# Where the modulation sums stand in the first attention of a two-layer decoder

## The chip, the cores and the metric

One core of a Trainium2 chip runs the whole forward pass of a two-layer decoder trunk as one program. The metric is the device time of one execution in microseconds. A core has five engines that run their own instruction queues in order and wait for each other by semaphores: TensorE (PE, matrix products), VectorE (DVE), ScalarE (ACT), GpSimd (POOL) and SyncE (SP, which here only issues DMAs).

## The reference, cut to what matters

The trunk works on 256 tokens of width 1024 in fp32. Every layer is a SwiGLU FFN, an attention, and another FFN; each sub-layer's input is normalised and modulated by a shift and a scale, and its output by a gate, which come from one vector `c`. Layer 0 uses differential attention with 8 heads, the stage of this study:

```python
c_act = jax.nn.silu(c)
mod = c_act @ ada_w[layer] + ada_b[layer]
sh1, sc1, g1, sh2, sc2, g2, sh3, sc3, g3 = jnp.split(mod, N_MOD, axis=-1)
...
h = modulate(rms_norm(x, norm_g[layer, 1]), sh2, sc2)
qkv = h @ w_qkv
...
logits = jnp.einsum('bqhmd,bkhmd->bhmqk', qb, k).astype(jnp.float32) * scale + bias
logits = jnp.where(rel >= 0, logits, -jnp.inf)
p = jax.nn.softmax(logits, axis=-1)
w = p[:, :, 0] - lam * p[:, :, 1]
return jnp.einsum('bhqk,bkhe->bqhe', w.astype(v.dtype), v)
...
o = rms_norm(o, subln_g) * (1 - lambda_init)
return o.reshape(b, s, A_V_WIDTH) @ w_o
```

The products `c_act @ ada_w` (18 sections of 1024 outputs over both layers, and two for the shared keys and values) don't depend on the tokens. They can be worked out at any time until the sub-layer that uses them.

## The kernel before, in words

**Products in three parts.** Activations are held transposed (feature on the partition, 256 tokens on the free axis). Each fp32 operand is split in a high and a low part of a faster type: `HH`/`HL` for activations, `wh`/`wl` for weights, and a product is three matmuls (`wh`·`HH`, `wl`·`HH`, `wh`·`HL`; `mm3`). A weight piece of 128 x 1024 comes from HBM into one of 6 `raw` tiles (SP issues the DMA), ACT makes `wh` (`cp_part`, a CAST), and DVE makes `wl` = raw - wh (`sub_part`, in one of 5 tiles). As soon as the subtraction is done, SP may load the next piece into that `raw` tile. A piece of 24 matmuls keeps PE busy for about 2.7 us.

**Modulation sums.** One modulation sum (`ada_block`) is one DVE instruction over a 128 x 1024 half of an `ada` tile, which multiplies by silu(c) and sums along the row: 128 outputs of a section. 160 of them are needed. Three `ada` tiles of 1 MB are kept; after the second half of a tile its next load is issued (`ada_dma`), in the same SP queue as the weights. `need(...)` makes whatever is still missing where a section is used; the first attention has to leave behind the sections (0,5), (0,6) and (0,7).

**What sets the order.** The engines' queues are written in program order by a planner inside the kernel. It keeps an estimated time per engine (`InOrder`). After each matmul, `work` calls `bg`, which gives ACT and DVE weight splitting and, in the mode "run", modulation sums for which a credit has built up; the credit grows with PE's work at the rate `PACE` of the stage (0.74 in the first attention). Before an instruction that would wait by the estimate, `fill_dve` and `fill_act` put the same kinds of work into the gap; `plain(f, ...)` writes an instruction sequence without such fillings, and `dve.plainly` one instruction.

**The first attention** (`attention_a`). `late_pairs` makes queries and keys of heads 0 and 1. Then, while PE works through the value projection (`v_proj`) and the other heads' query and key projections (`pair_proj`, 48 matmuls each, tile `pqk`), the heads go through a pipeline, one group per head. `group(t)` puts on PE the scores of head t (`s`), the transposes of head t-1's weights (`pw`), the value products of head t-2 and the transposes of head t-3's result (`po`). Behind that follow `exps(t)`: four reads of the scores by DVE (`nl`<-`s`,`g`, which add the bias and take the row's extreme `nm`), each followed by an exponential on ACT; `squares` on ACT and `inv_rms` (DVE row `ss`, then a power on POOL); and `out_split` (ACT `oh`, DVE `ol`). `combine(t)` forms the difference of the two softmaxes on DVE (a reciprocal and five scalings `rs`, `nl`), which PE transposes in the next group. `scale_o` scales the result on ACT (`on`). From head 7 on PE fills the time with the output projection (`OutProj`, tile also `pw`), and `finish` ends the stage with the update of x, whose halves feed the next FFN.

In before, only the reads of head 7 and its combination stand under `plain`: in the other heads `fill_dve` may put a `wl` or a sum between two reads.

Of the kernel before, what the change touches and what calls it, by code (L numbers as in the profile page):

```python
# [22 lines left out]
AH = 8  # L23
# [17 lines left out]
CP_FIT = 0.9  # L41
DVE_FIT = 0.6
NFILL = 1
PACE = [0.62, 0.74, 0.62, 0.38, 0.76, 0, 0.74]
NRAW = 6
NLO = 5
NHI = 6
# [57 lines left out]
def trunk(ctx, tc, a, out):  # L105
# [4 lines left out]
    dve = InOrder(tc, nc.vector, 0.08, 1 / 960)  # L110
# [17 lines left out]
    def bbank(name):  # L128
        return pp.tile([P, 512], F32, tag="tb", name=name)
# [3 lines left out]
    def plain(f, *args):  # L133

        r = []
        act.plainly(lambda: dve.plainly(lambda: r.append(f(*args))))
        return r[0]
# [40 lines left out]
    ada_at = {}  # L178
# [4 lines left out]
    ada_done = [0]  # L183
# [742 lines left out]
    def pair_proj(src, dst, name):  # L926

        pq = mmbank(name)
        blk = take(src)
        for k in range(NC):  # L930
            for b in range(2):
                mm3(pq[:, b * 256:b * 256 + 256], blk(k * 256 + b * P), hn[k],
                    k == 0 and b == 0, k == NC - 1)
            if k == NC - 1:
                act.copy(dst, pq)
            yield k, NC
# [37 lines left out]
    for k in range(0, NC, 2):  # L974
# [7 lines left out]
        if k % 4:  # L982
            i = k // 4
# [75 lines left out]

    pace[0] = PACE[0]  # L1060
    ffn(0, 0, None, ((0, 1), (0, 0)), ((0, 4), (0, 3)))
# [3 lines left out]
    def attention_a():  # L1065
# [7 lines left out]
        def qk_tile(hd):  # L1073
            return kp.tile([P, 512], F32, tag="w512a", name=f"qk{hd}")
# [4 lines left out]
        def load_g(hd):  # L1079
            g = cp_.tile([P, S], F32, tag=("hidh10", "hidl10")[hd % 2], name=f"g{hd}")  # L1080
            nc.gpsimd.dma_start(g, bass.AP(skew.tensor, skew.offset + hd * P * UW + 127, [[UW - 1, P], [1, S]]))
            gs[hd] = g
# [7 lines left out]
        def scores(hd):  # L1090
            sb = [sbank(f"s{hd}_{m}") for m in range(2)]
            for qt, (c0, w) in enumerate(QT):
                for m in range(2):
                    rows = slice(m * HD, m * HD + HD)
                    mm(sb[m][:, c0:c0 + w], qk[hd][rows, qt * P:qt * P + P], qk[hd][rows, 256:256 + w],
                       start=True, stop=True)
            return sb

        def exps(hd, sb):
            g = gs[hd]  # L1100
            nl = []
            nm = kp.tile([P, 4], F32, tag="nm", name=f"nm{hd}")
            sm = kp.tile([P, 4], F32, tag="sm", name=f"sm{hd}")
            for m in range(2):
                s = sb[m]
                n_ = cp_.tile([P, 384], F32, tag=f"hidh{4 + 2 * (hd % 2) + m}", name=f"nl{hd}_{m}")
                nl.append(n_)
                for qt, (c0, w) in enumerate(QT):
                    cc = 2 * m + qt
                    dve.tensor_tensor_reduce(  # L1110
                        n_[:, c0:c0 + w], s[:, c0:c0 + w], g[:, S - w:], -0.125, BIG,
                        ALU.add, ALU.min, accum_out=nm[:, cc:cc + 1])
                    act.activation(n_[:, c0:c0 + w], n_[:, c0:c0 + w], AF.Exp,
                                   bias=nm[:, cc:cc + 1], scale=-1.0,
                                   accum_out=sm[:, cc:cc + 1])
            st[hd], sms[hd] = nl, sm

        def combine(hd):
            nl, sm = st[hd], sms[hd]
            rs = kp.tile([P, 4], F32, tag="rs", name=f"rs{hd}")  # L1120
            dve.reciprocal(rs, sm)
            dve.tensor_scalar(rs[:, 2:4], rs[:, 2:4], nlam, None, op0=ALU.mult)
            for qt, (c0, w) in enumerate(QT):
                cs = slice(c0, c0 + w)
                dve.tensor_scalar(nl[1][:, cs], nl[1][:, cs], rs[:, 2 + qt:3 + qt], None, op0=ALU.mult)
                dve.scalar_tensor_tensor(nl[0][:, cs], nl[0][:, cs], rs[:, qt:qt + 1], nl[1][:, cs],
                                         op0=ALU.mult, op1=ALU.add)
            st[hd] = nl[0]
            if hd + 2 < AH:
                load_g(hd + 2)  # L1130

        def weights_t(hd):
            pw = abank(f"pw{hd}")
            for b in range(3):
                pe.transpose(pw[:, b * P:b * P + P], st[hd][:, b * P:b * P + P], ident)
            return pw

        def values(hd, po):
            wt = st[hd]
            vs = slice((hd % 4) * P, (hd % 4) * P + P)  # L1140
            v0, v1 = va[0][hd // 4][:, vs], va[1][hd // 4][:, vs]
            mm(po[:, 0:P], wt[:, 0:P], v0, start=True, stop=True)
            mm(po[:, P:2 * P], wt[:, P:2 * P], v0, start=True, stop=False)
            mm(po[:, P:2 * P], wt[:, 2 * P:3 * P], v1, start=False, stop=True)

        def squares(hd, po):
            on = kp.tile([P, 256], F32, tag="w512b", name=f"on{hd}")
            ss = kp.tile([P, 2], F32, tag="ss", name=f"ss{hd}")
            for qt in range(2):
                act.activation(on[:, qt * P:qt * P + P], po[:, qt * P:qt * P + P], AF.Square,  # L1150
                               accum_out=ss[:, qt:qt + 1])
            st[hd] = (po, on, ss)

        def inv_rms(hd):
            ss = st[hd][2]
            dve.tensor_scalar(ss, ss, 1.0 / P, EPS, op0=ALU.mult, op1=ALU.add)
            nc.gpsimd.tensor_tensor(ss, ss, half, op=ALU.pow)
            InOrder.ready[(ss.tensor.name, 0)] = dve.t + 1.0

        def scale_o(hd):  # L1160
            po, on, ss = st[hd]
            for qt in range(2):
                act.activation(on[:, qt * P:qt * P + P], po[:, qt * P:qt * P + P], AF.Copy,
                               scale=ss[:, qt:qt + 1])
            st[hd] = on

        def out_t(hd, pz):
            for qt in range(2):
                pe.transpose(pz[:, qt * P:qt * P + P], st[hd][:, qt * P:qt * P + P], ident)

        def out_split(hd, pz):
            oh, ol = o[hd]
            act.activation(oh, pz, AF.Identity, scale=subg)
            dve.scalar_tensor_tensor(ol, pz, subg, oh.bitcast(F32), op0=ALU.mult, op1=ALU.subtract)

        def group(t):

            hs, hw, hv, ho = (h if 0 <= h < AH else None for h in (t, t - 1, t - 2, t - 3))
            bank = bbank(f"po{t}") if hv is not None or ho is not None else None
            sb = scores(hs) if hs is not None else None  # L1180
            pw = weights_t(hw) if hw is not None else None
            if hv is not None:
                values(hv, bank[:, :256])
            if ho is not None:
                out_t(ho, bank[:, 256:])
            if hw is not None:
                wt = cp_.tile([P, 384], F32, tag=f"hidh{8 + hw % 2}", name=f"wt{hw}")
                act.copy(wt, pw[:, :384])
                st[hw] = wt
            if hs is not None:  # L1190
                plain(exps, hs, sb) if hs == AH - 1 else exps(hs, sb)
            if hv is not None:
                squares(hv, bank[:, :256])
                inv_rms(hv)
            if ho is not None:
                plain(out_split, ho, bank[:, 256:]) if ho == AH - 1 else out_split(ho, bank[:, 256:])

        def after(t):
            if t < AH:
                plain(combine, t) if t == AH - 1 else combine(t)  # L1200
            if 0 <= t - 2 < AH:
                scale_o(t - 2)

# [16 lines left out]
        for t in range(2, AH):  # L1220
            qk.append(qk_tile(t))
            for i, _ in enumerate(pair_proj("wqk", qk[t], f"pqk{t}")):
                if t > 2 and i == 2:
                    group(t - 1)
                if t > 2 and i == 5:
                    combine(t - 1)
                if t > 2 and i == 7:
                    scale_o(t - 3)
        step(4)
# [8 lines left out]

    pace[0] = PACE[1]
    op, rest = attention_a()  # L1240
    op.finish((0, 5), ((0, 7), (0, 6)), rest, (3, 2, 2, 1, 0, 0, 0, 0))
    pace[0] = PACE[2]
    ffn(0, 1, "late", ((0, 7), (0, 6)), (("kv", 1), ("kv", 0)), at=3)
# [10 lines left out]
    for t in fgs:  # L1254
        nc.gpsimd.memset(t.bitcast(F32), 0.0)
    pace[0] = PACE[3]
    rstd = late_pairs("wkk", kT, (("kv", 1), ("kv", 0)), AF.Exp)
# [54 lines left out]

    pace[0] = PACE[4]
    ffn(1, 0, "ready", None, ((1, 4), (1, 3)))
# [142 lines left out]

    pace[0] = PACE[5]
    op, rest = attention_b()
# [135 lines left out]
```

## Time and profile before

| | us |
|---|---|
| three runs, median (lowest to highest) | 965.37 (964.58 to 965.74) |
| the profiled execution | 964.25 |
| its span, first to last instruction | 962.5 |
| first attention in the span (chain: from the first lp to the last output projection) | 193.4 to 300.7 |
| 18 modulation sums in 193 to 300 us on DVE | 22.7, 1.28 each |
| 31 wl subtractions in 193 to 300 us on DVE | 37.0, 1.22 each |

A row of the view in order of time gives its start and length in us, engine, line, operation, output<-inputs, shapes, and in brackets the engine's idle time before it with what ended it. Rows of one engine overlap by some hundredths of a microsecond, so spacing is read from start to start. Nearly every instruction has the line 100, that of the helper which records it; the tiles' names tell them apart. Names in the profile have no buffer numbers: `nl` stands for all heads, and heads are told by the order. Matmuls are pipelined, their rows (0.28 us) overlap, and PE's time is read from the spacing: 0.11 us for 128 x 256.

### The profile page before, as it was taken

How to read it: one execution, taken by the hardware profiler on the slowest of the kernel's cores; microseconds unless marked ns; L12 is line 12 of the kernel's file. 1: busy time of each engine (PE TensorE's matmuls, PEld its weight loads, DVE VectorE, ACT ScalarE, POOL GpSimd, SP SyncE). 2: the span in 40 equal slices, each digit the busy share in tenths (PEclk: the TensorE clock that was granted, in tenths of full speed). 3: DMA queues.
4: the chain of work that ended last, by engine and by line, in shares of the span. 5: the costliest groups of instructions: out<-in, count | busy, mean ns of one | idle time of the engine just before them, and what ended most of it. 6: DMA issues, size and time to landing. Idle time of an engine off the chain costs nothing.

```text
span 962.5 us, 20495 instructions
## 1 busy us (share of the span) xinstructions
PE 953.4 (99%) x8088; PEld 930.1 (97%) x8088; DVE 821.8 (85%) x1369; ACT 556.4 (58%) x908; POOL 75.6 (8%) x119
## 2 busy tenths in 40 slices
PE   8999999999999999999999999999999999999997
PEld 7999999988999999999997999999998899999997
DVE  8989988889999999878899988889988799555575
ACT  6575654575877645455577554445567766554432
POOL 0000001100112000000000000000064014300000
PEclk9999999999999999999999999999999999999999
DMA  9998989968767699878959899989895437987641
GB/s 367 414 368 310 375 313 324 364 220 309 270 212 251 214 381 381 293 282 314 337 187 370 310 343 333 342 290 317 320 315 168 118 127 220 269 169 248 192 148 44
DMA packets 69661, 267.89 MB, mean 278 GB/s; under 512 B 9572, under 2 KB 10413, under 8 KB 59454
## 3 DMA queue, kind: packets, MB, share of 16 engines
q1 hardware_dynamic: 66060, 259.35, 76.9%
q0 software_dynamic: 3072, 6.92, 2.5%
q8 instruction: 63, 1.03, 0.4%
q10 hardware_dynamic: 434, 0.33, 0.1%
q14 instruction: 32, 0.26, 0.1%
HBM read 264.42 MB, written 2.66 MB: 277 GB/s over the span
## 4 chain that ended last, share of the span: by engine, by line
PE 98%; DVE 1%; DMA 0%; ACT 0%; issue 0%; SPq 0%; DVEq 0%; ACTq 0%
PE po L100 26%; PE pg L100 22%; PE pu L100 22%; PE pw L100 5%; PE pv L100 5%; PE pf L100 5%; PE lp L100 4%; PE pqk L100 3%; PE lq L100 1%; PE lu L100 1%; PE lg L100 1%; PE pk L100 1%; PE wb L100 1%; PE sb L100 1%; PE s L100 1%; PE wa L100 0%
## 5 line engine op out<-in xcount | busy, mean ns | idle before, releaser
L100 ACT CAST wh<-raw 128x1024 fp32r<-128x1024 f32 (+1 forms) x360 | 347.7, 975 | 206.7 <-PE pu L100 87.0
L100 DVE TENSOR_TENSOR wl<-raw,wh 128x1024 fp32r<-128x1024 f32 (+1 forms) x360 | 401.8, 1132 | 74.2 <-ACT sg L100 25.0
L100 DVE CUSTOM_DVE_ANT_0 ada<-ada,cact,vecs 128x1024 f32<-128x1024 f32 x144 | 182.7, 1279 | 0.0
L100 PE MATMUL pg<-HH,wl 128*128 128x256 f32 x608 | 167.9, 276 | 0.0
L100 PE MATMUL pu<-HH,wh 128*128 128x256 f32 x608 | 167.9, 276 | 0.0
L100 PE MATMUL pg<-HH,wh 128*128 128x256 f32 x608 | 167.9, 276 | 0.0
L100 PE MATMUL pu<-HL,wh 128*128 128x256 f32 x608 | 167.9, 276 | 0.0
L100 PE MATMUL pg<-HL,wh 128*128 128x256 f32 x608 | 167.9, 276 | 0.0
L100 PE MATMUL pu<-HH,wl 128*128 128x256 f32 x608 | 167.9, 276 | 0.0
L100 PE MATMUL po<-hidh,wh 128*128 128x256 f32 x528 | 145.7, 276 | 0.0
L100 PE MATMUL po<-hidh,wl 128*128 128x256 f32 x528 | 145.7, 276 | 0.0
L100 PE MATMUL po<-hidl,wh 128*128 128x256 f32 x528 | 145.7, 276 | 0.0
L100 PEld LDWEIGHTS pg<-HH,wh 128*128 128x128 f32 x608 | 114.1, 188 | 0.0
L100 PEld LDWEIGHTS pg<-HH,wl 128*128 128x128 f32 x608 | 114.1, 188 | 0.0
L100 PEld LDWEIGHTS pg<-HL,wh 128*128 128x128 f32 x608 | 114.1, 188 | 0.0
L100 PEld LDWEIGHTS pu<-HH,wh 128*128 128x128 f32 x608 | 114.1, 188 | 0.0
L100 PEld LDWEIGHTS pu<-HL,wh 128*128 128x128 f32 x608 | 114.1, 188 | 0.0
L100 PEld LDWEIGHTS pu<-HH,wl 128*128 128x128 f32 x608 | 114.1, 188 | 0.0
L100 PEld LDWEIGHTS po<-hidh,wl 128*128 128x128 f32 x528 | 99.1, 188 | 0.0
L100 PEld LDWEIGHTS po<-hidl,wh 128*128 128x128 f32 x528 | 99.1, 188 | 0.0
L100 PEld LDWEIGHTS po<-hidh,wh 128*128 128x128 f32 x528 | 99.1, 188 | 0.0
L100 ACT CAST hidh<-hf 128x512 fp32r<-128x512 f32 x44 | 27.3, 621 | 47.3 <-DVE hf L100 47.3
(244 smaller groups left out, 1878.3 us busy)
## 6 DMA issues: line engine op xcount, KB each, us to landing
raw<-in_win SPq DMA_DIRECT2D x176, 512.0 KB, 5.6
ada<-in_ada SPq DMA_DIRECT2D x79, 1024.0 KB, 7.3
raw<-in_wout SPq DMA_DIRECT2D x48, 384.0 KB, 5.4
raw<-in_wout SPq DMA_DIRECT2D x48, 320.0 KB, 5.1
raw<-in_wqk SPq DMA_DIRECT2D x16, 512.0 KB, 4.9
raw<-in_wo SPq DMA_DIRECT2D x16, 512.0 KB, 4.7
raw<-in_wlast SPq DMA_DIRECT2D x16, 512.0 KB, 4.3
raw<-in_wv SPq DMA_DIRECT2D x8, 512.0 KB, 8.1
```

Source lines behind the costliest of these rows:

```text
L100: return self.tc.keep_in_program_order(f(*args, **kw))
```

## The change

Every head's reads are now written under `plain`, so neither a wl nor a sum nor a CAST comes between them. The credit's rate in the first attention goes to 0, and a function `sums` writes up to two modulation sums, without a planner's condition other than that sections which this stage must leave behind are still missing. It is called behind the combinations of heads 0, 1 and 7 (`after`) and, in the loop over heads 2 to 7's projections, at step 5, which is behind `combine(t - 1)`; for t = 2 no combination stands there. That makes nine calls and 18 sums.

```diff
-PACE = [0.62, 0.74, 0.62, 0.38, 0.76, 0, 0.74]
+PACE = [0.62, 0, 0.62, 0.38, 0.76, 0, 0.74]
...
             if hs is not None:
-                plain(exps, hs, sb) if hs == AH - 1 else exps(hs, sb)
+                plain(exps, hs, sb)
...
+        due = 2 * max(ada_at[m] for m in ((0, 5), (0, 7), (0, 6)))
+
+        def sums():
+            for _ in range(2):
+                if ada_done[0] < due:
+                    dve.plainly(ada_block)
+
         def after(t):
             if t < AH:
                 plain(combine, t) if t == AH - 1 else combine(t)
+            if t in (0, 1, AH - 1):
+                sums()
             if 0 <= t - 2 < AH:
                 scale_o(t - 2)
...
                 if t > 2 and i == 5:
                     combine(t - 1)
+                if i == 5:
+                    sums()
                 if t > 2 and i == 7:
                     scale_o(t - 3)
```

PE's order is the same in both. DVE's differs from head 0's combination to the end of this stage and nowhere else. The first place is DVE around the reads of head 5. Before (the row `ISA nl..<-s..` is a read, `ISA ada` a sum, the short ISA rows write out an accumulator):

```order
L100 TENSOR_TENSOR wl<-raw,wh 128x1024
L100 ISA nl_0_3464,nm_3462<-s_0_3445,g_3286 128x128
L100 ISA nm_3462 128x1
L100 TENSOR_TENSOR wl<-raw,wh 128x1024
L100 ISA nl_0_3464,nm_3462<-s_0_3445,g_3286 128x256
L100 ISA nm_3462 128x1
L100 ISA nl_1_3473,nm_3462<-s_1_3446,g_3286 128x128
L100 ISA nm_3462 128x1
L100 ISA nl_1_3473,nm_3462<-s_1_3446,g_3286 128x256
L100 ISA nm_3462 128x1
L100 ISA ada,modall<-ada,cact,vecs 128x1024
L100 ISA modall 128x1
```

And now, from the end of head 4's combination on:

```order
L100 ISA ada,modall<-ada,cact,vecs 128x1024
L100 ISA modall 128x1
L100 ISA ada,modall<-ada,cact,vecs 128x1024
L100 ISA modall 128x1
L100 TENSOR_TENSOR wl<-raw,wh 128x1024
L100 ISA nl_0_3459,nm_3457<-s_0_3440,g_3277 128x128
L100 ISA nm_3457 128x1
L100 ISA nl_0_3459,nm_3457<-s_0_3440,g_3277 128x256
L100 ISA nm_3457 128x1
L100 ISA nl_1_3464,nm_3457<-s_1_3441,g_3277 128x128
L100 ISA nm_3457 128x1
L100 ISA nl_1_3464,nm_3457<-s_1_3441,g_3277 128x256
```

One sum behind the reads has become two ahead of them, and the second wl has moved from between the reads to behind them. The same holds for heads 6 and 7; head 4 has no wl between its sums and its reads.

The second place is DVE behind the combination of head 7 (its last two rows come first). Before:

```order
L100 TENSOR_SCALAR nl7_1_3691<-nl7_1_3691,rs7_3726 128x256
L100 SCALAR_TENSOR_TENSOR nl7_0_3686<-nl7_0_3686,rs7_3726,nl7_1_3691 128x256
L100 TENSOR_TENSOR wl_3760<-raw_3431,wh_3664 128x1024
L100 TENSOR_TENSOR wl_3786<-raw_3469,wh_3733 128x1024
L100 TENSOR_SCALAR ss6_3783<-ss6_3783 128x2
L100 SCALAR_TENSOR_TENSOR ol2_2596<-po8_3770,small_90,oh2_2592 128x256
```

Now:

```order
L100 TENSOR_SCALAR nl7_1_3688<-nl7_1_3688,rs7_3723 128x256
L100 SCALAR_TENSOR_TENSOR nl7_0_3683<-nl7_0_3683,rs7_3723,nl7_1_3688 128x256
L100 ISA ada_3394,modall_91<-ada_3394,cact_89,vecs_75 128x1024
L100 ISA modall_91 128x1
L100 SCALAR_TENSOR_TENSOR modall_91<-modall_91,vecs_75 128x4
L100 ISA ada_3394,modall_91<-ada_3394,cact_89,vecs_75 128x1024
L100 ISA modall_91 128x1
L100 TENSOR_TENSOR wl_3757<-raw_3417,wh_3570 128x1024
L100 TENSOR_SCALAR ss6_3785<-ss6_3785 128x2
L100 SCALAR_TENSOR_TENSOR ol2_2596<-po8_3770,small_90,oh2_2592 128x256
```

A pair of sums stands there where two wl stood. PE uses this `wl_3757` in the second row of a piece of the output projection, some twenty instructions behind head 7's transposes:

```order
L100 MATMUL pw3_3644<-oh1_2591,wh_3542 128x256
L100 MATMUL pw3_3644<-oh1_2591,wl_3697 128x256
L100 MATMUL pw3_3644<-ol1_2595,wh_3542 128x256
L100 MATMUL pw0_3641<-oh1_2591,wh_3570 128x256
L100 MATMUL pw0_3641<-oh1_2591,wl_3757 128x256
```

The third place is SP's queue at that time. Before, `raw_3659` is the piece whose CAST stands in ACT's queue between head 7's `squares` and its last scaling:

```order
L100 DMA ada_3483<-in_ada 128x2048
L100 DMA raw_3546<-in_wo 128x1024
L100 DMA raw_3584<-in_win 128x1024
L100 DMA raw_3659<-in_win 128x1024
L100 DMA raw_3702<-in_win 128x1024
```

Now that place in ACT's queue belongs to `raw_3759`:

```order
L100 DMA raw_3647<-in_wo 128x1024
L100 DMA raw_3699<-in_win 128x1024
L100 DMA ada_3733<-in_ada 128x2048
L100 DMA raw_3759<-in_win 128x1024
L100 DMA raw_3816<-in_win 128x1024
```

It is a later piece than before's, and the load of an `ada` tile stands right ahead of it.

## The prediction

> **What bounds the kernel now.** I read the page's busy shares first, then the chain of work that ended last, then the list of PE's waits, then the windows of this stage, and only after that the rows in order of time.
>
> ```profile
> PE 953.4 (99%) x8088; PEld 930.1 (97%) x8088; DVE 821.8 (85%) x1369; ACT 556.4 (58%) x908; POOL 75.6 (8%) x119
> PE 98%; DVE 1%; DMA 0%; ACT 0%; issue 0%; SPq 0%; DVEq 0%; ACTq 0%
> PE warm L100 <- DVE ones L100: 1.1, 1, 1.1
> PE psn L100 <- DVE sqs L100: 1.1, 1, 1.1
> PE pf L100 <- DVE wl L100: 0.2, 1, 0.2
> 193.00:245.00 52.00, 52.00 (x350) 46.16 (x348) 49.21 (x105) 36.30 (x76) 3.48 (x6) 1.00 0.77 275
> 245.00:300.00 55.00, 55.00 (x478) 52.71 (x479) 50.82 (x129) 42.50 (x125) 8.26 (x12) 1.00 0.75 255
> ```
>
> TensorE (PE) is the bound. It is busy 99% of the span, it carries 98% of the chain, and the list of its waits has three entries, 2.4 us in all, none of them in the first attention (193 to 300 us). The two windows (columns: PE, PEld, DVE, ACT and POOL busy, clock, DMA share, GB/s) show PE busy 52 of 52 and 55 of 55 us there. So nothing can be won: there is no wait of PE in this stage to remove. What the change can do is make PE wait, and the engine to watch is DVE, busy 49.21 and 50.82 us.
>
> **How the present order fits.** From head 3 to head 6 PE comes round every 7.68 us: the scores' matmuls start at 252.68 and 260.36 in the chain. DVE comes round in the same time, from the first read of the scores at 253.57 to that of the next head at 261.25, with one modulation sum (the ada row) in it.
>
> ```profile
> 252.68 0.86 PE s L100 x8
> 260.36 0.86 PE s L100 x8
> 253.57 0.29 DVE L100 CUSTOM_DVE_ANT_0 nl<-s,g 128x128 f32<-128x128 f32 x1
> 255.82 1.28 DVE L100 CUSTOM_DVE_ANT_0 ada<-ada,cact,vecs 128x1024 f32<-128x1024 f32 x1
> 261.25 0.29 DVE L100 CUSTOM_DVE_ANT_0 nl<-s,g 128x128 f32<-128x128 f32 x1
> ```
>
> There is next to nothing left in such a round, so a second sum in it does not fit. That is the whole of the forecast; the rest sizes it.
>
> **The change part by part.** The number of sums stays: 18 in this stage before, nine pairs after. Before, nine of them are done by the end of head 2's reading, four stand singly in heads 3 to 6, and five behind head 7. Now two stand behind every head's combination, and one more pair ahead of head 2. Of the reads themselves nothing is added.
>
> *The new round.* The last head of before already has the new order of rows (reads without work between, wl, ss, ol, combination), so its length is measured:
>
> ```profile
> 275.54 1.22 DVE L100 TENSOR_TENSOR wl<-raw,wh 128x1024 fp32r<-128x1024 f32 x1
> 276.68 0.28 DVE L100 CUSTOM_DVE_ANT_0 nl<-s,g 128x128 f32<-128x128 f32 x1
> 279.48 0.17 DVE L100 TENSOR_SCALAR ss<-ss 128x2 f32<-128x2 f32 x1 [0.48 <-ACT on L100]
> 279.77 0.48 DVE L100 SCALAR_TENSOR_TENSOR ol<-po,small,oh 128x256 fp32r<-128x256 f32 x1
> 281.61 0.49 DVE L100 SCALAR_TENSOR_TENSOR nl<-nl,rs,nl 128x256 f32<-128x256 f32 x1
> 282.02 2.36 DVE L100 TENSOR_TENSOR wl<-raw,wh 128x1024 fp32r<-128x1024 f32 x2
> 285.07 1.28 DVE L100 CUSTOM_DVE_ANT_0 ada<-ada,cact,vecs 128x1024 f32<-128x1024 f32 x1
> 287.48 1.28 DVE L100 CUSTOM_DVE_ANT_0 ada<-ada,cact,vecs 128x1024 f32<-128x1024 f32 x1
> ```
>
> From the first read to the end of the combination 276.68 to 282.02 is 5.34 us, with 0.48 of waiting for ACT in it. Two sums take 285.07 to 287.48, 2.41. One wl takes 275.54 to 276.68, 1.14. A new round is 5.34 + 2.41 + 1.14 = **8.89 us against PE's 7.68**: DVE falls back by 1.21 per head.
>
> *Where the falling back begins.* Head 2's scores start on PE at 237.34; read 0.9 later, as head 4's are (252.68 to 253.57), its combination ends at 238.2 + 5.34 = 243.6, and a pair of sums at 246.0. So head 3 is read there as before (245.89), with eight sums made instead of nine and one wl less. In head 3 ACT's first exponential starts at 246.75 in before and depends on PE's transposes, not on DVE. In head 7 the way from there (277.00) to ss (279.48) is 2.48 us, and from ss to the combination's end (282.02) 2.54. So head 3's combination ends at 246.75 + 2.48 + 2.54 = 251.77. Two sums follow, and a scaling of the modulation (from the sum's end at 289.89 to the next row at 290.09, 0.20): head 4 is read at 251.77 + 2.41 + 0.20 = 254.38, 0.8 later than before. With 8.89 per round head 5 is read at 263.27, head 6 at 272.16, head 7 at 281.05, where before read it at 276.68.
>
> ```profile
> 237.34 0.86 PE s L100 x8
> 245.89 0.29 DVE L100 CUSTOM_DVE_ANT_0 nl<-s,g 128x128 f32<-128x128 f32 x1
> 246.75 0.41 ACT L100 ACTIVATE nl<-nl,nm 128x128 f32<-128x128 f32 x1
> 277.00 0.40 ACT L100 ACTIVATE nl<-nl,nm 128x128 f32<-128x128 f32 x1
> 289.89 0.08 DVE L100 DVE_READ_ACCUMULATOR2_ANT modall<- 128x1 f32 x1
> 290.09 0.17 DVE L100 TENSOR_SCALAR ss<-ss 128x2 f32<-128x2 f32 x1
> ```
>
> *What PE asks for, and when.* The next rows are the wl that before makes for 263.23; PE's first use of the wl that the new order makes just ahead of heads 5, 6 and 7, then the three transposes of head 7's weights, the wl behind the last pair of sums, and the last transposes of this stage.
>
> ```profile
> 252.33 1.22 DVE L100 TENSOR_TENSOR wl<-raw,wh 128x1024 fp32r<-128x1024 f32 x1
> 263.23 0.28 PE L100 MATMUL pqk<-HH,wl 128*128 128x256 f32 x1
> 270.91 0.28 PE L100 MATMUL pqk<-HH,wl 128*128 128x256 f32 x1
> 278.59 0.28 PE L100 MATMUL pw<-oh,wl 128*128 128x256 f32 x1
> 282.22 0.49 PE L100 MATMUL pw<-tri,nl 128*128 128x128 f32 x3
> 285.33 0.28 PE L100 MATMUL pw<-oh,wl 128*128 128x256 f32 x1
> 291.75 0.44 PE L100 MATMUL po<-tri,on 128*128 128x128 f32 x2
> ```
>
> A wl is done 0.08 after the following row starts (1.22 long, 1.14 apart). So those three are done at 263.35, 272.24 and 281.13: 0.1, 1.3 and 2.5 us after PE's time. In before the first of them was made at 252.33, ten us ahead; that lead goes because heads 3 and 4 now make one wl each instead of two. These waits are steps on the way and are not added up: DVE's chain does not wait for PE here, so PE's lateness at any point is DVE's lateness there. Head 7's combination ends with a row that runs 281.61 to 282.10, 5.42 after the first read: 281.05 + 5.42 = 286.47. PE wants it with its second transpose, about 282.33 (three in 0.33 from 282.22). **First term: 4.1 us.**
>
> *Behind it.* DVE is free at 286.39; sums and scaling take 2.61, to 289.00; the wl is whole at 290.22. PE wants it at 285.33: 4.9 late. **Second term: 0.75 more.** Before, these sums stood at 285.07 behind two wl, which covered them; that cover is gone.
>
> *SP's queue and ACT's.* Each pair of sums frees an ada tile, so its 1 MB load is issued there, and one stands in SP's queue right ahead of the raw piece whose CAST stands in ACT's queue ahead of head 7's last scaling (on), for which PE waits in the row at 291.75.
>
> ```profile
> 289.65 1.06 ACT L100 CAST wh<-raw 128x1024 fp32r<-128x1024 f32 x1
> 291.06 0.63 ACT L100 ACTIVATE on<-po,ss 128x128 f32<-128x128 f32 x2 [0.36 <-POOL ss L1157]
> raw<-in_win SPq DMA_DIRECT2D x176, 512.0 KB, 5.6
> raw<-in_wv SPq DMA_DIRECT2D x8, 512.0 KB, 8.1
> ```
>
> That load waits for the wl that ends at 290.2. With the 5.6 us of the first DMA row the piece lands at 295.8, CAST and scaling (1.06 and 0.63, less 0.1 of overlap) end at 297.4; PE, 4.9 late, asks at 296.65. **Third term: 0.7**, between 0 (landing in 4.9 or less) and 3.2 (the 8.1 of the second row).
>
> *After the stage* DVE's order is the same row for row, and all of it waits for PE's later x, so I add nothing; what covers it is that PE leaves this stage as late as everything else.
>
> Sum: 4.1 + 0.75 + 0.7 = 5.55, call it 5.6. The profiled execution took 964.25 us (span 962.5 and 1.75 around it), so it would take 969.85. The median of the three runs, 965.37, lies 1.1 above it; I put the same 5.6 on the median: **971.0 us**, 0.6% slower.
>
> *A rule that bears on the steps.* The granted clock is 1.00 in both windows. The Trainium skill, page "TensorE: Matmul & The Clock Gate", section "HAM oscillation — how this bites in real kernels", says that PE must not stand idle for more than about 3.4 us, or its clock is halved. By that rule the 4.9 us would be harmless as the steps of 0.1 to 1.6 us that I work out, and would cost more as one standing; no run here shows such a drop.
>
> **The rivals.**
>
> *DVE's round is shorter, and it isn't slower.* The waits in the round (0.48 ahead of ss, 0.2 between ss and ol) are ACT's. If ACT answers at once when DVE runs behind PE, a round loses 0.68, five heads lose 3.4, and the sum falls to 4.1 + 0.75 - 3.4 = 1.5 us: 966.9, within 0.2%. It decides at about 0.55 of waiting saved per head. For it: ACT is busy only 42.50 of 55 us. Against: in head 7, where ACT's exponentials followed each read by 0.3 us, the waits stood all the same, since ACT's four exponentials and two squares simply take longer than DVE's reads and one wl.
>
> *The raw piece lands late.* If the load behind the ada tile takes 8.1 us, the third term is 3.2: 965.37 + 8.05 = 973.4. For it: the two loads are queued back to back. Against: DMA's share is 0.75 here.
>
> *PE's clock falls.* If the lateness came as one long standing and the clock were halved for one head's 48 matmuls (5.46 us in the chain), that would add 5.5: 976.5. This is the case of the rule above. It needs one standing of most of the 4.9; the three wl rows break it up.
>
> *Faster* would need PE to have time to give back, and it has none here: 965.4 at best. That the change doesn't do what it says is out: the rows of the new order show the pairs and the unbroken reads.
>
> **How the numbers follow.** Forecast 0.74 (969 to 972.5 by the third term's ends and some tenths on each round), raw piece late 0.09, clock 0.04, shorter round 0.11, faster 0.02. The range leaves out the shorter round, the clock and the faster case, 0.17 together: from 967.4 (about where the shorter round ends) to 973.8 (the late piece and some tenths). About 0.2%, 1.9 us, is what a measurement of this kernel can tell from no change. Slower by more: 0.74 + 0.09 + 0.04 = 0.87; within it 0.11; faster 0.02.
>
> **What would show it.** In the profile after: PE's waits now name DVE's wl and nl between 260 and 290 us; first reads of heads 4 to 7 about 8.9 us apart; two ada rows between each combination and the next wl; head 7's last combination row ends near 286.5; PE leaves the stage 5 to 6 us later and loses nothing behind it. It is wrong if the reads come 8.2 us apart or less, if PE's lateness before 282 us stays under 2 us, or if a wait appears behind 300 us.

## The result, and the profile after

| | before | after |
|---|---|---|
| median of 7 runs (lowest to highest), us | 965.37 (964.58 to 967.39) | 971.16 (970.00 to 976.32) |
| the profiled execution | 964.25 | 971.20 |
| its span | 962.5 | 969.5 |

The ratio is 1.0069 with a 95% interval of 1.0055 to 1.0082: slower by 5.3 to 7.9 us. The forecast was 971.0 and slower by 5.6.

The page of the changed kernel, busy shares and then the chain of work that ended last:

```profile
PE 956.8 (99%) x8088; PEld 932.5 (96%) x8088; DVE 823.6 (85%) x1369; ACT 556.8 (57%) x908; POOL 74.0 (8%) x119
PE 93%; DVE 3%; ACT 2%; DMA 1%; issue 0%; SPq 0%; ACTq 0%; DVEq 0%
```

DVE is busy 85% as before, and yet 3% of the chain has moved to it. The average over the span hides what is new. The list of PE's waits shows it (columns: who waits <- for whom, us in all, times, longest):

```profile
PE pw L100 <- DVE wl L100: 1.2, 2, 0.7
PE pw L100 <- DVE nl L100: 1.1, 2, 0.7
PE warm L100 <- DVE ones L100: 1.1, 1, 1.1
PE psn L100 <- DVE sqs L100: 1.0, 1, 1.0
PE po L100 <- ACT on L100: 0.8, 1, 0.8
PE pqk L100 <- DVE wl L100: 0.8, 1, 0.8
```

`warm` and `psn` stood in before's list too (they lie in the first 14 us). The other four are new and lie in the first attention: the `wl` ahead of the reads, head 7's weights, and the last scaling. The windows of this stage say the same:

```profile
193.00:245.00 52.00, 52.00 (x350) 46.29 (x349) 45.77 (x98) 35.77 (x76) 3.47 (x6) 1.00 0.76 280
245.00:300.00 55.00, 51.09 (x429) 47.39 (x428) 49.15 (x126) 38.00 (x115) 6.66 (x10) 1.00 0.66 240
```

Up to 245 us PE is busy throughout and DVE has some 3 us less to do than before (45.77 against 49.21). Afterwards PE stands: it is busy 51.09 of 55 us. DVE, busy 49.15 of 55, still looks as if it had time to spare. Part of it is a wait for ACT in every round (the row at 267.06 below), and rows behind that wait can't fill it, since they are done in order.

**A clock for the comparison.** The profiled execution of the changed kernel lost 0.99 us before the change begins. The first two rows are windows of it, the third is head 2's scores in its chain (before: 237.34), and the last two are the row with which the next FFN's normalisation starts, behind the stage, in before's chain and in the chain after:

```profile
9.00:11.00 2.00, 2.00 (x11) 2.00 (x12) 1.93 (x6) 1.64 (x3) 0.00 (x0) 0.52 1.09 412
11.00:13.00 2.00, 2.00 (x12) 1.81 (x12) 1.15 (x4) 0.44 (x2) 0.00 (x0) 0.63 0.97 401
238.33 0.86 PE s L100 x8
304.98 0.43 PE psn L100 x2
311.92 0.43 PE psn L100 x2
```

Between 9 and 13 us PE was granted 0.52 and 0.63 of its clock, where before shows 1.00 there. PE is 0.03 us late at 8.4 us, 0.97 at 14.4 and 0.99 at head 2's scores, so that is where the 0.99 comes from. Behind the stage PE is 6.94 late, so the stage lost **5.95 us**. To the end of the span (7.0) nothing is added.

**The round.** DVE in order of time: the first reads of heads 4 to 7, one whole round between heads 4 and 5, the end of head 7's combination and the wl behind it.

```profile
255.35 0.29 DVE L100 CUSTOM_DVE_ANT_0 nl<-s,g 128x128 f32<-128x128 f32 x1
260.70 1.28 DVE L100 CUSTOM_DVE_ANT_0 ada<-ada,cact,vecs 128x1024 f32<-128x1024 f32 x1
261.90 1.28 DVE L100 CUSTOM_DVE_ANT_0 ada<-ada,cact,vecs 128x1024 f32<-128x1024 f32 x1
263.11 1.23 DVE L100 TENSOR_TENSOR wl<-raw,wh 128x1024 fp32r<-128x1024 f32 x1
264.24 0.29 DVE L100 CUSTOM_DVE_ANT_0 nl<-s,g 128x128 f32<-128x128 f32 x1
267.06 0.17 DVE L100 TENSOR_SCALAR ss<-ss 128x2 f32<-128x2 f32 x1 [0.48 <-ACT on L100]
273.13 0.28 DVE L100 CUSTOM_DVE_ANT_0 nl<-s,g 128x128 f32<-128x128 f32 x1
282.02 0.28 DVE L100 CUSTOM_DVE_ANT_0 nl<-s,g 128x128 f32<-128x128 f32 x1
286.96 0.49 DVE L100 SCALAR_TENSOR_TENSOR nl<-nl,rs,nl 128x256 f32<-128x256 f32 x1
289.97 1.22 DVE L100 TENSOR_TENSOR wl<-raw,wh 128x1024 fp32r<-128x1024 f32 x1
```

264.24 - 255.35, 273.13 - 264.24 and 282.02 - 273.13 are 8.89 us each, three times the sum that the prediction made of rows of before. Not all of it is DVE's work: from 264.58 to 267.32 the chain runs over ACT, through the exponentials, the squares and `oh`, and the wl that DVE makes meanwhile is not in it. PE's own rows carry the lateness:

```profile
273.27 0.38 PE L100 MATMUL pqk<-HH,wl 128*128 128x256 f32 x1 [0.76 <-DVE wl L100]
282.16 0.39 PE L100 MATMUL pw<-oh,wl 128*128 128x256 f32 x1 [0.69 <-DVE wl L100]
287.50 0.44 PE L100 MATMUL pw<-tri,nl 128*128 128x128 f32 x2 [0.40 <-DVE nl L100]
291.24 0.39 PE L100 MATMUL pw<-oh,wl 128*128 128x256 f32 x1 [0.53 <-DVE wl L100]
298.57 0.44 PE L100 MATMUL po<-tri,on 128*128 128x128 f32 x2 [0.81 <-ACT on L100]
```

| PE's row | before | after | later, less 0.99 | forecast |
|---|---|---|---|---|
| first use of the wl ahead of head 5 | 263.23 | 264.39 | 0.17 | 0.1 |
| of the wl ahead of head 6 | 270.91 | 273.27 | 1.37 | 1.3 |
| of the wl ahead of head 7 | 278.59 | 282.16 | 2.58 | 2.5 |
| second transpose of head 7 | 282.33 | 287.50 | 4.18 | 4.1 |
| wl behind the last pair | 285.33 | 291.24 | 4.92 | 4.9 |
| last transposes | 291.75 | 298.57 | 5.83 | 5.6 |

A bracket (0.76, 0.69) is only the last wait ahead of that row; PE's lateness is read from the column "later", not by adding brackets. The last step stands in the chain and in ACT's rows:

```profile
291.25 5.62 DMA raw<-in_win
296.95 1.05 ACT L100 CAST wh<-raw 128x1024 fp32r<-128x1024 f32 x1 [1.23 <-DMA raw<-in_win]
297.90 0.61 ACT L100 ACTIVATE on<-po,ss 128x128 f32<-128x128 f32 x2
```

The wl ends at 291.19, its raw tile is loaded anew from 291.25 to 296.87, ACT stands 1.23 us for it, and the scaling behind it lets PE go on at 298.57.

### The profile page after: what moved, and what is told of

It is laid out like the page before. It is cut to its first block, busy times and chain, and to the rows that moved or that the text cites. A ratio compares the mean times of both kernels' runs of the same rounds, so it can differ in the third digit from the quotient of the medians.

```text
span 969.5 us, 20475 instructions
## 1 busy us (share of the span) xinstructions
PE 956.8 (99%) x8088; PEld 932.5 (96%) x8088; DVE 823.6 (85%) x1369; ACT 556.8 (57%) x908; POOL 74.0 (8%) x119
## 4 chain that ended last, share of the span: by engine, by line
PE 93%; DVE 3%; ACT 2%; DMA 1%; issue 0%; SPq 0%; ACTq 0%; DVEq 0%
PE po L100 25%; PE pg L100 21%; PE pu L100 21%; PE pv L100 5%; PE pf L100 5%; PE lp L100 4%; PE pw L100 3%; PE pqk L100 1%; DVE ada L100 1%; PE lq L100 1%; PE lg L100 1%; PE lu L100 1%; PE pk L100 1%; ACT nl L100 1%; PE wb L100 1%; PE sb L100 1%
```

## The experiments

Theory A is the prediction's: a second sum makes DVE's round longer than PE's. Theory B: the cost is the place, since unbroken reads push a wl back. Theory C: the `ada` loads stand at other places in SP's queue and hold up the weights. To see the stage apart from the start and from later stages, the last two columns give PE's time from head 0's scores (210.88 in before) to head 7's second transpose and to the `psn` behind the stage, each less that of before, from the order-of-time rows of the profiled execution. Each kernel's ratio is to runs of before made beside it.

| kernel | median, us | ratio (95%) | lost to head 7's transposes | lost in the stage |
|---|---|---|---|---|
| after | 971.16 | 1.0069 (1.0055 to 1.0082) | 4.18 | 5.95 |
| e1, sums of 128 columns | 964.97 | 0.9995 (0.9983 to 1.0006) | 0.01 | -0.23 |
| e2, last pair later | 970.33 | 1.0058 (1.0036 to 1.0080) | 4.17 | 4.17 |
| e3, one sum per head | 967.76 | 1.0015 (1.0000 to 1.0031) | 0.30 | 2.00 |
| e4, reads only | 977.84 | 1.0125 (1.0107 to 1.0144) | 0.00 | 12.15 |
| e5, pairs only | 970.24 | 1.0055 (1.0043 to 1.0067) | 4.89 | 4.78 |
| e6, three per head | 972.80 | 1.0088 (1.0073 to 1.0104) | 7.38 | 7.27 |
| e7, one wl ahead of the last pair | 969.23 | 1.0054 (1.0034 to 1.0075) | 4.20 | 4.22 |
| e8, one sum per head, spread | 965.50 | 1.0012 (1.0001 to 1.0022) | 0.61 | 0.51 |

### e1: the same rows, shorter sums

```diff
         dve.tensor_tensor_reduce(
-            t[:, i], t[:, i], cact, 1.0, bias, ALU.mult, ALU.add,
+            t[:, i, :w], t[:, i, :w], cact[:, :w], 1.0, bias, ALU.mult, ALU.add,
             accum_out=mt[:, j:j + 1])
+        dve.t += (D - w) / 960
```

`w` is 128 in `sums` and 1024 elsewhere; the last line keeps the planner's estimate. The orders of PE, DVE and SP are those of the changed kernel; in ACT's one CAST has moved ahead of a `qk` copy (266.0).

> This kernel leaves work out: the 18 sums of the first attention multiply and add 128 of their 1024 columns, so the modulation values of (0,5), (0,6) and (0,7) are not the whole sums; every row, every wait and every load stands where it stands in the changed kernel. Theory A (DVE's round is too long by the second sum's own time): a pair shrinks from 2.41 us to some 0.5, a round's work from 8.89 to some 7.0 us, below PE's 7.68, so DVE waits for PE again. Expected 965.4 us (964.5 to 966.5), reads of heads 4 to 7 about 7.7 us apart, and no wait of PE behind the first 15 us. Theory B (the cost is the place: reads without a wl between them put the wl late) and theory C (the ada loads stand at other places in SP's queue and hold up the raw pieces): both are untouched by the length of a sum, so 971.2 as the changed kernel.

DVE, a pair and the first reads of heads 5 and 6:

```profile
260.70 0.35 DVE L100 CUSTOM_DVE_ANT_0 ada<-ada,cact,vecs 128x128 f32<-128x128 f32 x1
262.52 0.29 DVE L100 CUSTOM_DVE_ANT_0 nl<-s,g 128x128 f32<-128x128 f32 x1
270.20 0.29 DVE L100 CUSTOM_DVE_ANT_0 nl<-s,g 128x128 f32<-128x128 f32 x1
```

The reads are 7.68 apart, PE's round, and the stage costs nothing more than in before. DVE's order, which reads are unbroken, and the places of the loads in SP's queue were left as they are in the changed kernel, so B and C fall as causes of their own: nothing of the loss is left when the sums are short. The -0.23 in the table is no gain of the order: from the last transposes on, e1's 72 matmuls of the output projection follow each other every 0.1135 us, before's every 0.1178, which is 0.30 us (see the last section).

### e2 and e7: the second and the third term

In e2 the pair behind head 7's combination is written at the next call of `after` (`sums(n)` writes n sums; the first part of the diff); in e7 it stays, with one wl ahead of it (the second part):

```diff
-            if t in (0, 1, AH - 1):
-                sums()
+            sums({0: 2, 1: 2, 7: 0, 8: 2, 9: 0}[t])
...
+            if t == AH - 1:
+                sub_part()
             if t in (0, 1, AH - 1):
                 sums()
```

> Head 7's pair of sums is made one step later, behind group(8)'s ol and two wl; the other eight pairs stay. Theory A with the prediction's three terms: reads of heads 4 to 7 still 8.89 us apart and head 7's combination as late as before (4.2 us of PE's time lost up to there), but the wl in front of which the pair stood (0.75) and the raw piece that is freed by it (0.7 predicted, 0.9 in the profile of the changed kernel) come in time: 971.2 - 1.6 = 969.6 us (969.0 to 970.2). If the late raw piece hangs on PE's lateness and not on the pair, only the 0.75 goes: 970.4. If the last pair costs nothing of its own: 971.2.

> The changed kernel with one wl moved ahead of head 7's pair of sums. The first term (4.2) stays. The wl comes 2.4 us earlier than PE's need is late, so the second term (0.75) goes. For the third: if only the raw piece that this wl frees is late (5.6 us of load from 291.2 to 296.9), it now lands 2.4 us earlier and the third term (0.9) goes as well: 971.2 - 1.6 = 969.6. If the last scaling is held as much by ss, which stands behind three wl on DVE and then goes to POOL, some 0.8 of the third term stays: 970.4. If the late wl were no cause, 971.2.

Both lose 4.2 us up to head 7's transposes, as the changed kernel does, and nothing behind them: 4.17 and 4.22 in the stage against 5.95. So 1.75 us hang on the pair that stands ahead of one wl. e7 tells the two readings of the third term apart: with the wl earlier no wait for `on` is left in PE's list, so it was the raw piece, and not `ss` behind three wl. The medians, 970.33 and 969.23, lie on both sides of the 969.6 expected; e2's is just outside its range of 969.0 to 970.2. Their intervals alone could not tell 969.6 from 970.4, so this reading rests on the profiles.

### e3 and e8: all reads unbroken, one sum per head

```diff
-            if t in (0, 1, AH - 1):
-                sums()
+            sums({0: 1, 1: 3, 7: 1, 8: 3, 9: 1}[t])
...
-                    sums()
+                    sums({2: 4, 3: 1, 4: 1, 5: 1, 6: 1, 7: 1}[t])
```

e8 has `8: 2` in the first and `3: 2` in the second table.

> All reads stay unbroken and all 18 sums stay, but they stand otherwise: nine by the end of head 2's place (one behind head 0, one that the credit still places, three behind head 1, four ahead of head 2), one behind each of heads 2 to 7, three behind group(8)'s ol. Theory A: one sum less per round gives 8.89 - 1.20 = 7.69 us against PE's 7.68, so DVE keeps up: 965.4 to 966.2 us, reads of heads 4 to 7 at 7.7 us, waits of PE under 0.5 us in all behind 15 us. Theory B (unbroken reads as such): the wl still stand behind the reads, so PE waits for wl as in the changed kernel: above 969.

> The kernel with one sum per head lost 1.5 us in its tail (profile: 0.7 for head 7's last scaling, 0.8 for a wl), where three sums stand in one go behind group(8)'s ol. Here the reads are unbroken as well and one sum stands behind each combination of heads 3 to 7, two behind head 2's, but behind group(8)'s ol stand two, and one a step later. Theory A: 965.4 to 966.3 us, waits of PE behind 15 us under 0.6 us in all. If unbroken reads cost something of their own: 967 or more, with PE waiting for wl between 245 and 290 us. Faster than before by more than 0.2% is not expected of any order here, since before has no wait of PE in this stage to win.

In e3 0.30 us is lost up to head 7, where the pairs lost 4.18, though its reads are unbroken too. But 1.7 us go behind, which was not expected: 967.76 lies above the 965.4 to 966.2 of theory A. PE's waits, then DVE and ACT in order of time:

```profile
PE pw L100 <- DVE wl L100: 0.8, 1, 0.8
PE po L100 <- ACT on L100: 0.7, 1, 0.7
290.50 1.28 DVE L100 CUSTOM_DVE_ANT_0 ada<-ada,cact,vecs 128x1024 f32<-128x1024 f32 x1
291.70 0.17 DVE L100 TENSOR_SCALAR ss<-ss 128x2 f32<-128x2 f32 x1
292.67 0.62 ACT L100 ACTIVATE on<-po,ss 128x128 f32<-128x128 f32 x2 [1.18 <-POOL ss L1157]
```

Head 7's `ss` waits on DVE behind the third of three sums in a row, POOL's power follows it, and ACT stands 1.18 us for that. It is the same rule on a smaller scale: DVE rows that PE needs soon stood behind sums that it needs late. e8 takes one of the three away from there. Its stage loses 0.51, and one wait of PE is left in it:

```profile
PE pw L100 <- DVE nl L100: 0.4, 1, 0.4
```

With a ratio of 1.0012 (1.0001 to 1.0022) e8 is at most 2.1 us above before and not below it: unbroken reads as such cost next to nothing, and win nothing.

### e4 and e5: each half of the change alone

e4 is before with this one line, and e5 is the changed kernel with the line undone:

```diff
-                plain(exps, hs, sb) if hs == AH - 1 else exps(hs, sb)
+                plain(exps, hs, sb)
```

> The other half alone: before, with every head's reads unbroken, the credit's rate as before and no written pairs. The credit then finds no place between heads 3 and 6; four sums come behind group(8)'s ol and eight in one go ahead of the update of x. Theory A: with no sum in heads 3 to 6 a round is 8.89 - 2.41 = 6.5 us, so no wait of PE between 245 and 290 us. The loss comes behind: eight sums from about 293.3 take 9.6 us where before has one, the first x row comes 8 us later than its 294.9, and the matrix products that wait for x and for the wl behind it are late: about 976 us (974 to 978), PE waiting for DVE's x and wl behind 295 us. Theory B: PE waits for wl between 245 and 290 us, 4 us or more.

> The other half of the change alone: pairs of sums behind the combinations and no credit in this stage, but the reads of heads 0 to 6 as before, with a wl or a sum between them where DVE would wait. The early heads take three sums more that way, so that the last pair stands behind head 6 and none behind head 7. Theory A (two sums per round, wherever the wl stands): heads 3 to 6 have two sums and two wl each, the same 8.89 us per round; laid end to end, head 7's combination comes 4.7 us late, and behind it nothing more is lost: 970.1 us (969.3 to 970.9), reads of heads 4 to 7 some 8.9 us apart. Theory B (the unbroken reads cost the time): they are broken here as in before, so 965.4.

e4 loses nothing up to head 7 and 12.15 us behind. A wait of PE, two windows (the clock is the third number from the end), two rows of PE and one of DVE:

```profile
PE pw L100 <- DVE x L100: 8.3, 1, 8.3
301.00:302.00 1.00, 0.00 (x0) 0.00 (x0) 0.00 (x0) 0.00 (x0) 0.00 (x0) 0.50 1.07 442
306.00:308.00 2.00, 1.97 (x9) 1.97 (x10) 1.61 (x5) 2.00 (x6) 0.18 (x1) 0.50 0.91 291
306.63 0.41 PE L100 MATMUL pw<-ol,wh 128*128 128x256 f32 x1
306.84 0.41 PE L100 MATMUL pw<-oh,wh 128*128 128x256 f32 x1
302.44 1.28 DVE L100 CUSTOM_DVE_ANT_0 ada<-ada,cact,vecs 128x1024 f32<-128x1024 f32 x1 [1.99 <-DMA ada<-in_ada]
```

The eight sums in one go were foreseen. What they drag along was not. They use up the three `ada` tiles faster than these are loaded (DVE stands 1.99 us for one), and PE's standing of 8.3 us costs it half its clock: 0.50 from 300.8 to 311.0 us, matmuls 0.21 apart instead of 0.113. From 306.0 to 310.9 that is half of 4.9 us, some 2.4 more. 8.3 + 2.4 + 1.1 (a wait for wl) are 11.8 of the 12.15. So without places in the gaps of the reads the credit finds none in heads 3 to 6, and unbroken reads need sums that are written in; e3 and e8 show that one per head is enough.

e5 loses 4.89 us up to head 7, where the whole change loses 4.18. It is a weaker test of B than was meant: before has a wl between the reads of each of heads 3 to 6, of these e5 has one only in heads 3 and 5. What rules B out is e1, e3, e4 and e8, where every head's reads are unbroken and at most 0.61 us is lost up to head 7. First reads of heads 4 to 7 are 7.75, 8.85 and 9.09 apart; the 7.75 is head 5's, whose wl stands behind its first read. PE stands elsewhere on the way, for 1.9 of 3.9 us ahead of the scores, since ACT is held by the later reads and copies `qk` late:

```profile
269.28 0.93 PE L100 MATMUL s<-qk 64*128 64x128 f32 x8 [1.11 <-ACT qk L100]
```

The place of PE's waits depends on the order; with two sums in each round PE falls back by over 4 us in either.

### e6: three sums per head

```diff
-            if t in (0, 1, AH - 1):
-                sums()
+            if t == 1:
+                sums(1)
...
-                    sums()
+                    sums(2 if t == 2 else 3)
```

> Three sums behind each of the combinations of heads 2 to 5, one behind head 6's, the other five earlier; 18 as before, reads unbroken, none behind head 7. Theory A: each sum beyond the one that fits lengthens a round by 1.20, so 8.89 + 1.20 = 10.09 us in four heads and 7.68 in the last: DVE falls back by 2.41 per round instead of 1.21; laid end to end PE stands 7.4 us in all: 972.8 us (971.5 to 974). If it were the pairs' place and not their length, or a wait that comes once, it would stay near the 970 of the kernels without a late last pair.

First reads of heads 4, 5 and 6 on DVE:

```profile
257.11 0.29 DVE L100 CUSTOM_DVE_ANT_0 nl<-s,g 128x128 f32<-128x128 f32 x1
267.20 0.28 DVE L100 CUSTOM_DVE_ANT_0 nl<-s,g 128x128 f32<-128x128 f32 x1
277.49 0.28 DVE L100 CUSTOM_DVE_ANT_0 nl<-s,g 128x128 f32<-128x128 f32 x1
```

10.09 and 10.29 us apart (a scaling of the modulation stands in the second). 7.38 us are lost up to head 7, where 7.4 were expected. With e3 (one sum, 0.30) and the change (two, 4.18) that is a series. Behind heads 2 to 6 the change has five sums more than one per head and e6 eight; the three between them are 3.6 us of DVE and cost PE 3.2. A round that fits in 7.68 costs next to nothing.

One thing in e6 was not foreseen. A row of PE with the wait ahead of it, and a window right behind:

```profile
267.34 0.55 PE L100 MATMUL pqk<-HH,wl 128*128 128x256 f32 x1 [2.60 <-DVE wl L100]
267.50:270.50 3.00, 3.00 (x15) 3.00 (x16) 2.41 (x9) 2.73 (x13) 0.82 (x2) 0.50 1.00 397
```

PE stood 2.60 us and was then granted half its clock from 267.4 to 270.8. Half of 3.4 us is 1.7 us of PE's work (an estimate). It does not add to the 7.38: DVE's chain runs on without PE, and PE's next wait for a wl is only 0.70 us. So the near agreement with 7.4 stands for DVE's round, and the clock's fall was hidden under it.

## Why the prediction was right

**What bounds, and which engine to watch.** PE, and DVE: all new waits of PE end in rows of DVE or behind them.

**The round.** 5.34 + 2.41 + 1.14 = 8.89 was forecast and 8.89 measured, three times over. The last head of before stood in the new order already, waits for ACT included, and that made the sum exact. e1, e3 and e6 show that the loss up to head 7 follows this length.

**Where it begins.** Head 4's first read was forecast at 254.38; it came at 255.35, less 0.99 at 254.36.

**First term, 4.1.** The combination's end was forecast at 286.47; 286.96 + 0.49 less 0.99 is 286.46. PE was 4.18 late there.

**Second term, 0.75.** The wl was forecast whole at 290.22 and was at 290.20 (289.97 + 1.22 less 0.99). PE's lateness rose from 4.18 to 4.92. e2 and e7 take it away.

**Third term, 0.7 between 0 and 3.2.** The load took 5.62 where 5.6 was put in, and PE lost 0.9. The path (wl, raw tile, load, CAST, scaling) is the one in the chain, and e7 excludes the other one.

**Behind the stage.** Nothing forecast, nothing measured: 5.83 at the last transposes, 5.95 at the `psn`, 6.0 over the span.

**The rivals.** The shorter round fell with the row at 267.06: ACT's 0.48 stands ahead of `ss` when DVE runs late, too. The late piece did not come. The clock stayed at 1.00 in both windows although PE lost 5.95 us, in single waits of at most 0.8. But the prediction set the bar for this rival too high when it asked for one standing of most of the 4.9: in e6 a wait of 2.60 us was followed by 3.4 us at half the clock, and in e4 one of 8.3 us by some 10 us. The Trainium skill, page "TensorE: Matmul & The Clock Gate", section "HAM oscillation — how this bites in real kernels", puts the limit at gaps of PE of more than about 3.4 us. The changed kernel's stage and e4 fit that, but e6 does not: its clock fell behind a gap of 2.60 us, so here the limit lies lower than the page says, and where is open.

How near 971.0 and 971.16 lie is partly luck: the terms come to 5.55 and the profile to 5.95, while the ratio leaves 5.3 to 7.9.

## What to carry to other kernels

Where a pipeline comes round once per item, work out the round of every engine from one measured round in the new order, waits included; background work fits as long as this stays under the round of the bounding engine, and beyond that costs its excess times the number of rounds, however idle the engine's busy share looks. Spread such work one piece per round and do the rest where there is slack, early rather than in one go. And ask of each piece what stands right behind it: late work ahead of a row that is needed soon, or ahead of one that frees a buffer, is paid once more.

## What the runs showed of the hardware

**The clock at the start.** Two profiles (after and e7) show PE's clock at half for 3.4 us, from about 9 us on; the others show 1.00 there. It costs about 1 us and is no effect of the change, which begins 200 us later. No single wait of PE in the list of after is above 1.1 us. A difference of spans is only worth as much as a common landmark in both.

**A slower pace at full clock.** A 128 x 256 matmul follows the one before it every 0.1133 us in most stretches, but every 0.1178 in some, at a granted clock of 1.00 and with PE busy throughout. e7's profiled execution took 975.85 us, 6.6 above its median. Its stage and start are as told; 6.1 us come behind, in one FFN. Windows of before and of e7 there:

```profile
350.00:400.00 50.00, 50.00 (x443) 50.00 (x443) 45.96 (x60) 25.46 (x30) 0.00 (x0) 1.00 0.97 367
350.00:400.00 50.00, 50.00 (x427) 50.00 (x426) 45.27 (x60) 22.99 (x28) 0.00 (x0) 1.00 0.96 361
```

PE is busy throughout at a granted clock of 1.00 in both, and yet makes 427 matmuls instead of 443. By their starts they follow each other every 0.1178 us instead of 0.1133, evenly from about 330 us to the FFN's end, and in the next FFN every 0.1133 again. e7 has the longest such stretch, but every profile has some. In e2 and e3 it holds from 24.4 to 47 us, where before makes 202 matmuls and e2 197 (before's window, then e2's):

```profile
24.00:47.00 23.00, 23.00 (x202) 23.00 (x201) 23.00 (x34) 12.60 (x20) 0.00 (x0) 1.00 1.02 414
24.00:47.00 23.00, 23.00 (x197) 23.00 (x196) 23.00 (x34) 12.50 (x20) 0.00 (x0) 1.00 1.02 413
```

The 72 matmuls of the output projection behind the last transposes are at 0.1178 in before, in after and in most experiments, and at about 0.1136 in e1 and e3. So differences of some 0.3 us in the table can be this pace and not the order. Two of the seven runs of the changed kernel (975.31 and 976.32) lie some 5 us above the rest. Whether that was a long stretch of it can't be said, since only one execution of each kernel is profiled; what sets the pace stays open.
